# A kernel with a product-key expert layer: gates of all token groups made for all experts in one pass, their high and low parts laid out one behind the other

## The chip, the cores and the metric

The kernel runs on one core of a Trainium2 chip. The metric is the device time of one execution in microseconds. Of the kernel before there are three timed runs (1705.65, 1706.34 and 1710.72 us, median 1706.34) and one profiled execution of 1709.14 us, whose trace gives all rows below.

## The reference

One sequence of 256 tokens with 1024 features goes through a first block (a recurrent mixer, then an expert layer) and a second one (two layers of attention and a gated feed-forward). Only the expert layer matters here:

```
q     = t @ w_q                          # 256 tokens, 8 heads, 2 halves of 128
s, i  = top_k(q . sub_keys, 16)          # per half: 16 of 128 keys
idx   = i1 * 128 + i2  of the 16 best sums per head       # 128 experts per token, of 16384
g     = softmax(best)
out_p = sum over (h, k) of  g * gelu(u_tab[idx] . t_p) * v_tab[idx]
```

The kernel does not gather. It computes gelu(u . t) for all 16384 experts and all 256 tokens, multiplies by a gate that is zero where an expert was not chosen, and multiplies the result by all of v_tab. An expert is named by two numbers, i1 (0 to 127) and i2 (0 to 127): block i of the tables holds the 128 experts with i1 = i, and i2 is the partition.

## The kernel before, in words

**Weights.** All matrices come as 128x1024 fp32 tiles in one fixed list (`order`), 533 in all, each by one DMA on SP's queue (`w_dma`, L181). Each is split in two: ACT copies it to a high part (`whi`, L206), DVE subtracts to get the low part (`wlo`, L207). A product then has three matmuls: high by high, low by high, high by low (`mm3` L226, `add_part` L251). `weight(key)` (L218) hands out the next tile and splits those that follow, up to three tiles ahead while the u blocks run.

**The order of the work.** Python emits the instructions, and a planner that simulates the engines at build time places them in each engine's queue; every queue then runs in order on the chip. `tc.issue_after(x)` keeps an instruction behind x. `pump_behind(n)` (L808) takes n steps of a background generator and keeps what it emits behind the latest split of a weight.

**The u stage** (L959 to L967). For each of 128 blocks i, `u_block(i)` makes u tile i: 24 matmuls of 256 columns into one PSUM bank, gelu by ACT, and the result goes to row i of H (128 x 128 x 256 fp32, in three tiles: rows 0 to 31, 32 to 63, 64 to 127). In the first half of this stage the background is the choice of the experts (`topk`). When it ends, at about block 60, the background becomes `gates()`, in `pace` steps per block.

**Gates.** For a group of TB = 8 tokens: `one_hot` (L866) makes two 0/1 tables on DVE in fp16, with the 128 chosen experts of a token on the partitions: `eb` says which i2 each has, `ea` which i1. `with_gates` (L875) multiplies `ea` by the gate of each chosen expert, kept as a high and a low fp16 part, into `ahl`. On TensorE, `eb` of one token is the stationary operand and `ahl` of that token the moving one; the product is the gate of all (i2, i1) of the token. Tokens lie in pairs (TI = 2) as the innermost index of these tables.

Before the change the 32 groups are treated in two ways. In `gates()` groups 0 to 15 (tokens 0 to 127) are made for all 128 rows i1, and groups 16 to 31 for rows 0 to 63 only. `ahl` is laid out [group of pairs, row, high/low, token of the pair]: for one token and one part, the moving columns lie 4 fp16 elements, 8 bytes, apart. High and low are two matmuls that add up in PSUM (L886). `gate_apply` (L888) takes the gates from PSUM to H: rows whose u block is already there are multiplied by DVE (L893), the others are written by ACT (L896), and `u_block` multiplies them later by DVE (L954). A group is three background steps (four for groups 0 to 15); the steps are spread over the blocks up to 125:

```python
pace = (3 * T // TB + GM + 1) / (125 - i)      # L966: 113 steps, GM = 16
```

**The v stage** (L968 to L1003). H rows are split pairwise into a high and a low part (`ring`, L337 by ACT and L338 by DVE) and multiplied by the v tiles: 12 matmuls of 512 columns per row into four accumulating banks (L255). The ring lies where the u stage's input `xn2h`, `xn2l` was. The background of its first 64 rows is `gates_rest()` (L921): groups 16 to 31 for rows 64 to 127. It makes `eb` again, makes the other half of `ea` and of `ahl`, and here one matmul takes high and low together (L933): 64 rows x 2 parts = 128 moving columns, 2 elements, 4 bytes, apart, not added up in PSUM. ACT takes the low half out (L935), DVE adds the high half (L937) and multiplies H (L939).

Of the kernel before, what the change touches and what calls it, by code (L numbers as in the profile page):

```python
# [10 lines left out]
F32 = mybir.dt.float32  # L11
F32R = mybir.dt.float32r
F16 = mybir.dt.float16
# [3 lines left out]
AF = mybir.ActivationFunctionType  # L17
OP = mybir.AluOpType
# [3 lines left out]
T = 256  # L22
# [6 lines left out]
GS = 1024.0  # L29
TB = 8  # L30
TI = 2
NW = 3
HV = 36
PK = 1.35
GM = 16
LEAD = 4
VN = {"d": 1, "f": 0}
UL = (2, 7, 12, 17)
# [21 lines left out]
def kernel(  # L60
# [25 lines left out]
    pe, dve, act, pool = nc.tensor, nc.vector, nc.scalar, nc.gpsimd  # L86
# [22 lines left out]
    pacc = Four()  # L109
# [121 lines left out]
    def bank(shape, name, dt=F32):  # L231
        return pw.tile(shape, dt, tag="w", name=name)
# [92 lines left out]
    def background(gen):  # L325
        bgs["gen"], bgs["acc"] = gen, 0.0

    def pump(n):
        bgs["acc"] += n
        while bgs["acc"] >= 1.0:  # L330
            bgs["acc"] -= 1.0
            if bgs["gen"] is None or next(bgs["gen"], bgs) is bgs:
                bgs["gen"], bgs["acc"] = None, 0.0
                return
# [32 lines left out]
    IN_H0 = ("x", "yb", "lru", "sg")  # L367
    gp = pctx.enter_context(tc.tile_pool(name="gp", bufs=2))
    sks = []
    for tag, n, b in (("eb", 4, 2), ("ea", 4, 1), ("gs", 4, 1)):  # L370
        for j in range(b):
            t = gp.tile([128, n, 128], F32, tag=tag, name=f"sk{tag}{j}", bufs=b)
            sks += [(t, q, len(sks)) for q in range(n)]
    with tc.tile_pool(name="b1", bufs=1) as b1, tc.tile_pool(name="w1", bufs=1) as w1:
# [9 lines left out]
        x = full("x")  # L384
# [36 lines left out]
        r = raws.pop(0)  # L421
# [42 lines left out]
        for c in range(8):  # L464
            if c >= XG:
# [7 lines left out]
                                     op0=OP.mult, op1=OP.subtract)  # L473
# [7 lines left out]
        o = _OFF["norm2_g"]  # L481
# [79 lines left out]
        for c in range(8):  # L561
            if c % 4 == 0:
                Wg = weight(("ax", c // 4))
            o = (c % 4) * 256
# [93 lines left out]
        for c in range(8):  # L658
# [3 lines left out]
                                     op1=OP.subtract)  # L662
# [4 lines left out]
    with pctx:  # L667
        hp = pctx.enter_context(tc.tile_pool(name="hp", bufs=1))
        iE = gp.tile([128, 128, TI], F16, name="iE", bufs=1)
        i1T = gp.tile([128, T], F16, name="i1T", bufs=1)  # L670
        i2T = gp.tile([128, T], F16, name="i2T", bufs=1)

        gT = gp.tile([128, T // TI, 2, TI], F16, name="gT", bufs=1)
# [139 lines left out]
        for c in range(17):  # L813
# [10 lines left out]
            if c >= 2 and c % 2 == 0 and c <= 16:  # L824
                k = c // 2 - 1
                t = gp.tile([128, T], F32, tag="ut", name=f"x2t{k}")
# [11 lines left out]

        Hs = []
        HR = (0, 32, 64, 128)  # L840
        ub = {"u": 0, "groups": 0}

        def H_part(k):
            while len(Hs) <= k:
# [5 lines left out]
        def H_rows(a, b):  # L850

            for k in range(3):
                lo, hi = max(a, HR[k]), min(b, HR[k + 1])
                if lo < hi:
                    yield H_part(k)[:, (lo - HR[k]) * T:(hi - HR[k]) * T].rearrange("p (i t) -> p i t", t=T), lo, hi - lo

        def H_at(i, n=1):
            return next(H_rows(i, i + n))[0]

        TG = TB // TI  # L860

        def spread(row, t0, n):

            return row[:, t0:t0 + TB].rearrange("p (g j) -> p g j", j=TI).unsqueeze(2).to_broadcast([128, TG, n, TI])

        def one_hot(t0, a, n):  # L866
            eb = gp.tile([128, TG, 128, TI], F16, tag="eb", name=f"eb{a}_{t0}", bufs=2)
            dve.tensor_tensor(eb, spread(i2T, t0, 128), iE.unsqueeze(1).to_broadcast([128, TG, 128, TI]),
                              op=OP.is_equal)
            ea = gp.tile([128, TG, n, TI], F16, tag="ea", name=f"ea{a}_{t0}", bufs=1)  # L870
            dve.tensor_tensor(ea, spread(i1T, t0, n),
                              iE[:, a:a + n, :].unsqueeze(1).to_broadcast([128, TG, n, TI]), op=OP.is_equal)
            return eb, ea

        def with_gates(t0, a, n, ea):  # L875
            ahl = gp.tile([128, TG, n, 2, TI], F16, tag="ahl", name=f"ahl{a}_{t0}")
            dve.tensor_tensor(ahl, ea.unsqueeze(3).to_broadcast([128, TG, n, 2, TI]),
                              gT[:, t0 // TI:t0 // TI + TG].unsqueeze(2).to_broadcast([128, TG, n, 2, TI]),
                              op=OP.mult)
            return ahl  # L880

        def gate_sums(gps, eb, ahl):
            for t in range(TB):
                g, j = t // TI, t % TI
                for q in range(2):
                    pe.matmul(gps[:, t, :], eb[:, g, :, j], ahl[:, g, :, q, j], start=q == 0, stop=q == 1)  # L886

        def gate_apply(gps, t0, a, b):  # L888

            m = min(max(ub["u"], a), b)  # L890
            for hv, r, n in H_rows(a, m):
                hv = hv[:, :, t0:t0 + TB]
                dve.scalar_tensor_tensor(hv, gps[:, :, r - a:r - a + n].rearrange("p t i -> p i t"), 1.0 / GS, hv,  # L893
                                         op0=OP.mult, op1=OP.mult)
            for hv, r, n in H_rows(m, b):
                act.activation(hv[:, :, t0:t0 + TB], gps[:, :, r - a:r - a + n].rearrange("p t i -> p i t"), AF.Copy,  # L896
                               scale=1.0 / GS)

        def gates():

            pend = None
            for k in range(T // TB):
                t0, n = k * TB, 128 if k < GM else 64
                eb, ea = one_hot(t0, 0, n)
                yield
                ahl = with_gates(t0, 0, n, ea)
                yield
                if k < GM:
                    yield
                gps = pacc.tile([128, TB, n], F32, tag="g", name=f"g{t0}")  # L910
                gate_sums(gps, eb, ahl)
                if pend:
                    gate_apply(*pend)
                    ub["groups"] += 1
                pend = (gps, t0, 0, n)
                yield
            gate_apply(*pend)
            ub["groups"] += 1
            yield

        def gates_rest():  # L921
            for t0 in range(GM * TB, T, TB):
                eb, ea = one_hot(t0, 64, 64)
                yield
                ahl = with_gates(t0, 64, 64, ea)
                yield

                gs = gp.tile([128, 64, TB], F32, tag="gs", name=f"gs{t0}", bufs=1)
                for h in range(2):
                    gps = bank([128, 4, 64, 2], f"h{t0}{h}")  # L930
                    for t in range(4):
                        g, j = (4 * h + t) // TI, t % TI
                        pe.matmul(gps[:, t], eb[:, g, :, j], ahl[:, g, :, :, j], start=True, stop=True)  # L933
                    gv = gps.rearrange("p t i q -> p q i t")
                    act.activation(gs[:, :, 4 * h:4 * h + 4], gv[:, 1], AF.Copy)  # L935
                    yield
                    dve.tensor_tensor(gs[:, :, 4 * h:4 * h + 4], gv[:, 0], gs[:, :, 4 * h:4 * h + 4], op=OP.add)  # L937
                hv = H_at(64, 64)[:, :, t0:t0 + TB]
                dve.scalar_tensor_tensor(hv, gs, 1.0 / GS, hv, op0=OP.mult, op1=OP.mult)  # L939
                yield  # L940

        def u_block(i):
            W = weight(("u", i))
            ps = bank([128, T], f"u{i}")
            if i < 12:
                proj(ps, W, x2h, x2l)
            else:
                proj(ps, W, xn2h, xn2l)
            h = H_at(i)[:, 0, :]
            n = TB * (ub["groups"] if i < 64 else min(ub["groups"], GM))  # L950
            if n:
                t = gp.tile([128, T], F32, tag="ut", name=f"ut{i}")
                act.activation(t[:, 0:n], ps[:, 0:n], AF.Gelu_apprx_tanh)  # L953
                dve.tensor_tensor(h[:, 0:n], t[:, 0:n], h[:, 0:n], op=OP.mult)  # L954
            if n < T:
                act.activation(h[:, n:], ps[:, n:], AF.Gelu_apprx_tanh)  # L956
            ub["u"] = i + 1

        pace = PK  # L959
        for i in range(128):  # L960
            u_block(i)
            pump_behind(pace)
            if bgs["gen"] is None and pace == PK:
                pacc.hold(2)
                background(gates())
                pace = (3 * T // TB + GM + 1) / (125 - i)  # L966
        pump(1000)  # L967
        pacc.hold()  # L968
        background(gates_rest())
        acc = new_acc("pv")  # L970
        pairs = {}
        ring = [xp.tile([128, 4, 2, T], F32R, name=f"ring{x}", tag="x" + x) for x in "hl"]
# [23 lines left out]
        n_v = next(i for i, o in enumerate(order) if o[0] == ("v", 0))  # L996
        w_stage(n_v + HV, [in_h0(j) for j in range(4)])
        for i in range(125):
            if i == 64:
                pump(1000)  # L1000
            p = gated(i)
            W = weight(("v", i))
            add_k(acc, W, p, i == 0, False)  # L1003
            pump(5 * (T // TB - GM) / 56)
        Hr = hp.tile([128, 8192], F32, tag="H1", name="Hr")
        hk = Hr[:, 0:2048].rearrange("p (a b) -> p a b", a=2)
        nc.sync.dma_start(Hr[:, 0:2048], hdram)
# [28 lines left out]
    with ExitStack() as b2ctx:  # L1036
# [348 lines left out]
        h, xh, xl = layer_norm(acc, tail, h3, 0, 1, rows1, scales=r3a)  # L1385
# [199 lines left out]
```

## Time and profile before

| | |
|---|---|
| median of three runs | 1706.34 us |
| profiled execution, span in the trace | 1709.14 us, 1707.4 us |
| TensorE (PE), VectorE (DVE), ScalarE (ACT) busy | 1666.7, 1229.4, 902.1 us |
| u stage with gates | 441.3 to 676.7 us |
| v stage with the rest of the gates | 676.7 to 845.5 us |

Times in the rows count from the start of the span. PE is the matmul stream of TensorE, PEld its loading of stationary operands. [...] L12 is line 12 of the code.

### The profile page before, as it was taken

What the parts mean: (1) busy time and instruction counts of PE and PEld (TensorE: products, weight loads), DVE (VectorE), ACT (ScalarE), POOL (GpSimd) and SP (SyncE); (2) the same over time, 40 slices, a digit from 0 to 9 for tenths busy, and PEclk for the clock granted to TensorE, in tenths of its full rate; (3) what the DMA queues carried; (4) which work ended last, traced back from release to release, by engine and by line L of the source; (5) the groups of instructions that cost most, each with busy time, mean ns of one, the idle gap of its engine ahead of it and who ended that gap; (6) DMA issues with size and microseconds to landing.
All of it is one profiled execution on the core that took longest, in us unless ns stands there. A gap on an engine that the chain in (4) does not pass through costs nothing.

```text
span 1707.4 us, 29521 instructions
## 1 busy us (share of the span) xinstructions
PE 1666.7 (98%) x11533; PEld 1525.5 (89%) x11533; DVE 1229.4 (72%) x2220; ACT 902.1 (53%) x1556; POOL 121.6 (7%) x104
## 2 busy tenths in 40 slices
PE   8999999999999999999999999989999999999997
PEld 8998899999999999777788888877999889889997
DVE  7969689989777878778755546776766665567665
ACT  6786565454544444545544444765655456555552
POOL 2013010113000000000000001331000000000000
PEclk9999999999999999999999999999999999999999
DMA  7655646665544454556766655633765554346551
GB/s 245 199 161 163 208 147 222 187 186 180 167 146 140 149 154 145 189 180 204 240 193 190 194 188 198 194 105 106 228 188 186 170 174 137 111 143 217 183 185 50
DMA packets 90284, 296.61 MB, mean 174 GB/s; under 512 B 9168, under 2 KB 20000, under 8 KB 89376
## 3 DMA queue, kind: packets, MB, share of 16 engines
q1 hardware_dynamic: 88800, 293.66, 54.4%
q8 instruction: 91, 1.49, 0.4%
q10 hardware_dynamic: 1344, 1.05, 0.2%
q14 instruction: 49, 0.40, 0.1%
HBM read 289.39 MB, written 3.19 MB: 171 GB/s over the span
## 4 chain that ended last, share of the span: by engine, by line
PE 87%; DVE 5%; ACT 4%; DMA 2%; issue 2%; POOL 1%; POOLq 0%; SPq 0%; ACTq 0%; DVEq 0%
PE pv L255 21%; PE u L229 7%; PE u L227 7%; PE u L228 7%; PE ff L255 6%; PE g L886 3%; PE fg L229 2%; PE fg L227 2%; PE fg L228 2%; PE fu L227 2%; PE fu L229 2%; PE fu L228 2%; DVE wlo L207 1%; PE dpv L255 1%; PE ul L1132 1%
## 5 line engine op out<-in xcount | busy, mean ns | idle before, releaser
L207 DVE TENSOR_TENSOR wlo<-raw,whi 128x1024 fp32r<-128x1024 f32 x383 | 475.2, 1242 | 201.3 <-ACT whi L206 197.2
L206 ACT ACTIVATE whi<-raw 128x1024 fp32r<-128x1024 f32 x383 | 405.2, 1059 | 227.0 <-PE pv L255 87.3
L207 DVE TENSOR_TENSOR W<-raw,W 128x1024 fp32r<-128x1024 f32 x150 | 186.1, 1243 | 122.8 <-ACT W L206 122.5
L227 PE MATMUL u<-xn2h,whi 128*128 128x256 f32 x928 | 263.4, 284 | 0.0
L229 PE MATMUL u<-xn2l,whi 128*128 128x256 f32 x928 | 263.1, 284 | 0.0
L228 PE MATMUL u<-xn2h,wlo 128*128 128x256 f32 x928 | 262.7, 283 | 0.0
L206 ACT ACTIVATE W<-raw 128x1024 fp32r<-128x1024 f32 x150 | 158.7, 1061 | 155.5 <-PE pv L255 53.9
L228 PEld LDWEIGHTS u<-xn2h,wlo 128*128 128x128 f32 x928 | 175.5, 189 | 0.0
L227 PEld LDWEIGHTS u<-xn2h,whi 128*128 128x128 f32 x928 | 175.3, 189 | 0.0
L229 PEld LDWEIGHTS u<-xn2l,whi 128*128 128x128 f32 x928 | 175.1, 189 | 0.0
L255 PE MATMUL pv<-W,ringh 128*128 128x512 f32 x384 | 106.3, 391 | 0.0
L956 ACT ACTIVATE H<-u 128x256 f32<-128x256 f32 (+13 forms) x128 | 44.2, 345 | 92.6 <-PE u L229 92.5
L255 PE MATMUL pv<-whi,ringh 128*128 128x512 f32 x288 | 91.8, 399 | 0.1
L255 PE MATMUL pv<-whi,ringl 128*128 128x512 f32 x288 | 91.7, 395 | 0.0
L255 PE MATMUL pv<-wlo,ringh 128*128 128x512 f32 x288 | 89.8, 395 | 0.0
L255 PEld LDWEIGHTS pv<-W,ringh 128*128 128x128 f32 x384 | 71.6, 188 | 14.9
L953 ACT ACTIVATE ut<-u 128x128 f32<-128x128 f32 (+15 forms) x62 | 15.4, 248 | 123.9 <-PE u L229 123.9
L255 PEld LDWEIGHTS pv<-whi,ringl 128*128 128x128 f32 x288 | 54.1, 188 | 12.8
L255 PEld LDWEIGHTS pv<-wlo,ringh 128*128 128x128 f32 x288 | 53.9, 188 | 12.6
L255 PEld LDWEIGHTS pv<-whi,ringh 128*128 128x128 f32 x288 | 53.1, 188 | 11.8 <-ACT ringh L337 0.3
L255 PE MATMUL ff<-W,fph 128*128 128x512 f32 x192 | 59.3, 398 | 1.1 <-ACT fph L337 1.1
L255 PE MATMUL pv<-W,ringl 128*128 128x512 f32 x192 | 59.3, 390 | 0.0
(863 smaller groups left out, 4351.0 us busy)
## 6 DMA issues: line engine op xcount, KB each, us to landing
raw<-in_uT_dram SPq DMA_DIRECT2D x128, 512.0 KB, 3.6
raw<-in_v_dram SPq DMA_DIRECT2D x128, 512.0 KB, 3.6
raw<-in_ff_in_dram SPq DMA_DIRECT2D x80, 512.0 KB, 3.6
raw<-in_w_in_dram SPq DMA_DIRECT2D x56, 512.0 KB, 4.1
raw<-in_ff_out_dram SPq DMA_DIRECT2D x44, 512.0 KB, 4.1
raw<-in_w_q_dram SPq DMA_DIRECT2D x16, 512.0 KB, 3.6
raw<-in_qkw_dram SPq DMA_DIRECT2D x16, 512.0 KB, 4.1
raw<-in_f_qk_dram SPq DMA_DIRECT2D x16, 512.0 KB, 4.3
```

The source lines that it names most:

```text
L206: st["hi"] = act.activation(hi, r, AF.Copy).ins
L207: st["lo"] = dve.tensor_tensor(lo, r, hi.bitcast(F32), op=OP.subtract).ins
L227: pe.matmul(o, w[0], x[0], start=start, stop=False, skip_group_check=True)
L228: pe.matmul(o, w[1], x[0], start=False, stop=False, skip_group_check=True)
L229: pe.matmul(o, w[0], x[1], start=False, stop=stop, skip_group_check=True)
L255: i = pe.matmul(acc[2 * tt + nh], x_[:, ts], w_[:, nh * 512:nh * 512 + 512], start=f, stop=l, skip_group_check=True)
L886: pe.matmul(gps[:, t, :], eb[:, g, :, j], ahl[:, g, :, q, j], start=q == 0, stop=q == 1)
L953: act.activation(t[:, 0:n], ps[:, 0:n], AF.Gelu_apprx_tanh)
L956: act.activation(h[:, n:], ps[:, n:], AF.Gelu_apprx_tanh)
L1132: done = pe.matmul(u, x_[:, k, ts], w_[:, ns], start=f, stop=l, skip_group_check=True).ins
```

## The change

`gates_rest()` goes. `gates()` makes every group for all 128 rows beside the u blocks. `ahl` becomes [group of pairs, high/low, row, token of the pair], so that the columns of one part lie 2 elements, 4 bytes, apart; high and low stay two matmuls that add up in PSUM. Every group has three steps, 97 steps in all. `u_block` multiplies the gates of all tokens that are ready (`ub["gated"]`), in every row; before, at most 128 tokens in rows from 64 on. The 2 KB tile of `gates_rest` keeps its place in the pool under another name.

```diff
@@ -32,7 +32,6 @@
 NW = 3
 HV = 36
 PK = 1.35
-GM = 16
 LEAD = 4
 VN = {"d": 1, "f": 0}
 UL = (2, 7, 12, 17)
@@ -367,7 +366,7 @@
     IN_H0 = ("x", "yb", "lru", "sg")
     gp = pctx.enter_context(tc.tile_pool(name="gp", bufs=2))
     sks = []
-    for tag, n, b in (("eb", 4, 2), ("ea", 4, 1), ("gs", 4, 1)):
+    for tag, n, b in (("eb", 4, 2), ("ea", 4, 1), ("sk", 4, 1)):
         for j in range(b):
             t = gp.tile([128, n, 128], F32, tag=tag, name=f"sk{tag}{j}", bufs=b)
             sks += [(t, q, len(sks)) for q in range(n)]
@@ -838,7 +837,7 @@
 
         Hs = []
         HR = (0, 32, 64, 128)
-        ub = {"u": 0, "groups": 0}
+        ub = {"u": 0, "gated": 0}
 
         def H_part(k):
             while len(Hs) <= k:
@@ -863,81 +862,50 @@
 
             return row[:, t0:t0 + TB].rearrange("p (g j) -> p g j", j=TI).unsqueeze(2).to_broadcast([128, TG, n, TI])
 
-        def one_hot(t0, a, n):
-            eb = gp.tile([128, TG, 128, TI], F16, tag="eb", name=f"eb{a}_{t0}", bufs=2)
-            dve.tensor_tensor(eb, spread(i2T, t0, 128), iE.unsqueeze(1).to_broadcast([128, TG, 128, TI]),
-                              op=OP.is_equal)
-            ea = gp.tile([128, TG, n, TI], F16, tag="ea", name=f"ea{a}_{t0}", bufs=1)
-            dve.tensor_tensor(ea, spread(i1T, t0, n),
-                              iE[:, a:a + n, :].unsqueeze(1).to_broadcast([128, TG, n, TI]), op=OP.is_equal)
-            return eb, ea
-
-        def with_gates(t0, a, n, ea):
-            ahl = gp.tile([128, TG, n, 2, TI], F16, tag="ahl", name=f"ahl{a}_{t0}")
-            dve.tensor_tensor(ahl, ea.unsqueeze(3).to_broadcast([128, TG, n, 2, TI]),
-                              gT[:, t0 // TI:t0 // TI + TG].unsqueeze(2).to_broadcast([128, TG, n, 2, TI]),
+        def one_hot(t0):
+            e = [gp.tile([128, TG, 128, TI], F16, tag=f"e{x}", name=f"e{x}{t0}", bufs=n) for x, n in (("b", 2), ("a", 1))]
+            for o, row in zip(e, (i2T, i1T)):
+                dve.tensor_tensor(o, spread(row, t0, 128), iE.unsqueeze(1).to_broadcast([128, TG, 128, TI]),
+                                  op=OP.is_equal)
+            return e
+
+        def with_gates(t0, ea):
+            ahl = gp.tile([128, TG, 2, 128, TI], F16, tag="ahl", name=f"ahl{t0}")
+            dve.tensor_tensor(ahl, ea.unsqueeze(2).to_broadcast([128, TG, 2, 128, TI]),
+                              gT[:, t0 // TI:t0 // TI + TG].unsqueeze(3).to_broadcast([128, TG, 2, 128, TI]),
                               op=OP.mult)
             return ahl
 
-        def gate_sums(gps, eb, ahl):
-            for t in range(TB):
-                g, j = t // TI, t % TI
-                for q in range(2):
-                    pe.matmul(gps[:, t, :], eb[:, g, :, j], ahl[:, g, :, q, j], start=q == 0, stop=q == 1)
-
-        def gate_apply(gps, t0, a, b):
-
-            m = min(max(ub["u"], a), b)
-            for hv, r, n in H_rows(a, m):
-                hv = hv[:, :, t0:t0 + TB]
-                dve.scalar_tensor_tensor(hv, gps[:, :, r - a:r - a + n].rearrange("p t i -> p i t"), 1.0 / GS, hv,
-                                         op0=OP.mult, op1=OP.mult)
-            for hv, r, n in H_rows(m, b):
-                act.activation(hv[:, :, t0:t0 + TB], gps[:, :, r - a:r - a + n].rearrange("p t i -> p i t"), AF.Copy,
-                               scale=1.0 / GS)
+        def gate_apply(gps, t0):
+
+            for a, b in ((0, ub["u"]), (ub["u"], 128)):
+                for hv, r, n in H_rows(a, b):
+                    hv, gv = hv[:, :, t0:t0 + TB], gps[:, :, r:r + n].rearrange("p t i -> p i t")
+                    if a:
+                        act.activation(hv, gv, AF.Copy, scale=1.0 / GS)
+                    else:
+                        dve.scalar_tensor_tensor(hv, gv, 1.0 / GS, hv, op0=OP.mult, op1=OP.mult)
+            ub["gated"] = t0 + TB
 
         def gates():
 
             pend = None
-            for k in range(T // TB):
-                t0, n = k * TB, 128 if k < GM else 64
-                eb, ea = one_hot(t0, 0, n)
+            for t0 in range(0, T, TB):
+                eb, ea = one_hot(t0)
                 yield
-                ahl = with_gates(t0, 0, n, ea)
+                ahl = with_gates(t0, ea)
                 yield
-                if k < GM:
-                    yield
-                gps = pacc.tile([128, TB, n], F32, tag="g", name=f"g{t0}")
-                gate_sums(gps, eb, ahl)
+                gps = pacc.tile([128, TB, 128], F32, tag="g", name=f"g{t0}")
+                for t in range(TB):
+                    g, j = t // TI, t % TI
+                    for q in range(2):
+                        pe.matmul(gps[:, t, :], eb[:, g, :, j], ahl[:, g, q, :, j], start=q == 0, stop=q == 1)
                 if pend:
                     gate_apply(*pend)
-                    ub["groups"] += 1
-                pend = (gps, t0, 0, n)
+                pend = (gps, t0)
                 yield
             gate_apply(*pend)
-            ub["groups"] += 1
             yield
-
-        def gates_rest():
-            for t0 in range(GM * TB, T, TB):
-                eb, ea = one_hot(t0, 64, 64)
-                yield
-                ahl = with_gates(t0, 64, 64, ea)
-                yield
-
-                gs = gp.tile([128, 64, TB], F32, tag="gs", name=f"gs{t0}", bufs=1)
-                for h in range(2):
-                    gps = bank([128, 4, 64, 2], f"h{t0}{h}")
-                    for t in range(4):
-                        g, j = (4 * h + t) // TI, t % TI
-                        pe.matmul(gps[:, t], eb[:, g, :, j], ahl[:, g, :, :, j], start=True, stop=True)
-                    gv = gps.rearrange("p t i q -> p q i t")
-                    act.activation(gs[:, :, 4 * h:4 * h + 4], gv[:, 1], AF.Copy)
-                    yield
-                    dve.tensor_tensor(gs[:, :, 4 * h:4 * h + 4], gv[:, 0], gs[:, :, 4 * h:4 * h + 4], op=OP.add)
-                hv = H_at(64, 64)[:, :, t0:t0 + TB]
-                dve.scalar_tensor_tensor(hv, gs, 1.0 / GS, hv, op0=OP.mult, op1=OP.mult)
-                yield
 
         def u_block(i):
             W = weight(("u", i))
@@ -947,7 +915,7 @@
             else:
                 proj(ps, W, xn2h, xn2l)
             h = H_at(i)[:, 0, :]
-            n = TB * (ub["groups"] if i < 64 else min(ub["groups"], GM))
+            n = ub["gated"]
             if n:
                 t = gp.tile([128, T], F32, tag="ut", name=f"ut{i}")
                 act.activation(t[:, 0:n], ps[:, 0:n], AF.Gelu_apprx_tanh)
@@ -963,10 +931,9 @@
             if bgs["gen"] is None and pace == PK:
                 pacc.hold(2)
                 background(gates())
-                pace = (3 * T // TB + GM + 1) / (125 - i)
+                pace = (3 * T // TB + 1) / (125 - i)
         pump(1000)
         pacc.hold()
-        background(gates_rest())
         acc = new_acc("pv")
         pairs = {}
         ring = [xp.tile([128, 4, 2, T], F32R, name=f"ring{x}", tag="x" + x) for x in "hl"]
@@ -996,12 +963,9 @@
         n_v = next(i for i, o in enumerate(order) if o[0] == ("v", 0))
         w_stage(n_v + HV, [in_h0(j) for j in range(4)])
         for i in range(125):
-            if i == 64:
-                pump(1000)
             p = gated(i)
             W = weight(("v", i))
             add_k(acc, W, p, i == 0, False)
-            pump(5 * (T // TB - GM) / 56)
         Hr = hp.tile([128, 8192], F32, tag="H1", name="Hr")
         hk = Hr[:, 0:2048].rearrange("p (a b) -> p a b", a=2)
         nc.sync.dma_start(Hr[:, 0:2048], hdram)
```

## Rows read from the trace of the kernel before

**Rows 1.** The page: busy time, share of the span, instructions of each engine

```profile
PE 1666.7 (98%) x11533; PEld 1525.5 (89%) x11533; DVE 1229.4 (72%) x2220; ACT 902.1 (53%) x1556; POOL 121.6 (7%) x104
```

**Rows 2.** Stretches: start and end, busy time (instructions) by engine, granted clock, DMA

```profile
core 0: us, PE busy (x) PEld busy (x) DVE busy (x) ACT busy (x) POOL busy (x), PEclk, DMA share, GB/s
300.00:350.00 50.00, 50.00 (x424) 50.00 (x423) 46.90 (x130) 23.61 (x36) 10.18 (x6) 1.00 0.61 190
441.30:676.70 235.40, 235.40 (x2099) 233.80 (x2097) 181.85 (x309) 98.02 (x209) 0.00 (x0) 1.00 0.48 149
640.00:676.00 36.00, 36.00 (x350) 35.72 (x350) 29.28 (x54) 14.87 (x31) 0.00 (x0) 1.00 0.52 158
676.70:845.50 168.80, 168.69 (x818) 134.15 (x817) 134.81 (x186) 91.09 (x128) 0.00 (x0) 1.00 0.62 191
```

**Rows 3.** Chain of waits, 441.3 to 676.7: shares; pieces (start, us, what)

```profile
by line: PE u L229 26.9%; PE u L228 26.9%; PE u L227 26.9%; PE g L886 19.3%
...
448.14 1.87 PE g L886 x16
...
574.71 1.87 PE g L886 x16
581.37 0.96 PE g L886 x16
...
600.68 0.97 PE g L886 x16
601.65 0.17 PE u L227
...
671.78 0.96 PE g L886 x16
```

**Rows 4.** Chain of waits, 676 to 845.5: shares; pieces

```profile
by line: PE pv L255 94.8%; PE h L933 4.4%; ACT ringh L337 0.4%; PE u L228 0.2%; PE u L227 0.1%; PE u L229 0.1%; issue 0.0%
...
676.87 0.64 ACT ringh L337
...
678.75 0.49 PE h L933 x8
...
842.11 0.25 PE h L933 x4
```

**Rows 5.** Line 956, 255 to 441.3: count, min/median/max ns, first and last start

```profile
L956 ACT ACTIVATE H<-u x61: 384/386/388, 267.9 to 438.8; 128x256 f32<-128x256 f32 x61
```

**Rows 6.** Timeline: start us, us, engine, line, operation [idle before]

```profile
441.32 0.68 DVE L868 TENSOR_TENSOR eb<-i2T,iE 128x1024 f16<-128x1024 f16 x1
441.92 0.68 DVE L871 TENSOR_TENSOR ea<-i1T,iE 128x1024 f16<-128x1024 f16 x1
...
460.01 1.22 DVE L877 TENSOR_TENSOR ahl<-ea,gT 128x2048 f16<-128x2048 f16 x1
461.15 1.22 DVE L207 TENSOR_TENSOR wlo<-raw,whi 128x1024 fp32r<-128x1024 f32 x1
462.29 0.75 DVE L893 SCALAR_TENSOR_TENSOR H<-g,H 128x256 f32<-128x256 f32 x2
...
463.72 2.03 PE L886 MATMUL g<-ahl,eb 128*128 128x128 f16 x16
...
667.73 0.29 DVE L954 TENSOR_TENSOR H<-ut,H 128x128 f32<-128x128 f32 x1
667.94 0.68 DVE L877 TENSOR_TENSOR ahl<-ea,gT 128x1024 f16<-128x1024 f16 x1
```

**Rows 7.** Waits, 441 to 680: who waited for whom, us, times, longest

```profile
DVE wlo L207 <- ACT whi L206: 33.9, 49, 2.4
DVE H L954 <- ACT ut L953: 21.2, 30, 1.2
```

**Rows 8.** Waits, 300 to 350

```profile
DVE wlo L207 <- ACT whi L206: 2.5, 5, 0.9
```

## The prediction

> **What bounds the kernel now.** I read the page first: TensorE is busy 98% of the span, VectorE (DVE) 72%, ScalarE 53% [rows 1]. A share over the whole span says little, so the second look is the table of stretches around the gates. [...] So in both stages TensorE sets the time, and what counts is what the gates cost in its stream. That is read from the chain of waits, the third look: u matmuls and gate matmuls alone make up the first stage, with the gates at 19.3% [rows 3], and in the second the gate matmuls hold 4.4% [rows 4]. The fourth look is at what DVE waits for, because the change puts work on it: there are 33.9 us of waits for the high part of a weight and 21.2 us for a gelu [rows 7].
>
> **Gate matmuls in the u stage.** A group is 16 matmuls. With 128 columns 8 bytes apart it takes 1.87 us of the chain, and there are 16 of these; with 64 columns 8 bytes apart 0.96, also 16 [rows 3]. The v stage has the shape that the change makes everywhere: 128 columns 4 bytes apart, 8 matmuls in 0.49 us, so 16 in 0.98 [rows 4]. That gives 117, 60 and 61 ns for one matmul. After the change all 32 groups are of the third kind, with one difference: its pairs add up in PSUM. The u matmuls add up in one bank too and take 0.12 us for 256 columns (66 blocks in 235.40 us less the 45.4 us of gates are 190.0 us, 1584 matmuls), 0.47 ns a column, as the 61 ns for 128 do; so I charge nothing for adding up. The first 16 groups save 16 x (1.87 - 0.98) = 14.2 us, the others lose 16 x 0.02 = 0.3: **-13.9 us**. The bounds of a new group are 0.96 (as many loads of the stationary operand, half the columns) and 1.87 (the layout does nothing); I take 0.98, the row of the same width and step.
>
> [...]
>
> **Gate matmuls in the v stage.** They go, 23 runs in the chain from 678.75 to 842.11: 4.4% of 168.8 us is **-7.4 us**. One run of eight lies beside the wait for the first ring tile (ScalarE, 0.64 us, which starts when the last u matmul has read the tile that the ring overwrites), so that wait stays and the run returns nothing [rows 4]. Also gone there are 16 groups of DVE and ScalarE work (tables, products, sums). TensorE did not wait for them, so they return nothing more.
>
> **DVE in the u stage.** This is the bill. I take distances from start to start. `eb` and a full `ea` take 0.60 each; `ahl` with 2048 elements 1.14; a weight's low part (1024 fp32 elements) 1.14, 0.08 under its shown duration; two pieces of gates on 256 elements 0.75 - 0.08, so 0.33 each; the product H<-ut with 128 tokens 0.21 [rows 6]. From 0.21 at 128 and 1.14 at 1024 elements I estimate 0.08 + 0.00104 per fp32 element. One u block takes (438.8 - 267.9) / 60 = 2.85 us without gates [rows 5]. Of the 128 blocks 61 are done when the first table is made [rows 5, 6], so the new pace is 97 steps over some 65 blocks, 1.49 a block, so a group comes every 2.0 blocks: 2.0 x 2.85 + 0.98 + 0.05 (the first u matmul after a group takes 0.17 us of the chain, not 0.12 [rows 3]) = 6.75 us of TensorE.
>
> DVE's share of that, per group: tables and `ahl` 2.34; the gates of r finished rows 0.33 + 0.33 + 0.08 + 0.0083 (r - 64); two low parts 2.28; two H products of n tokens 2 x (0.08 + 0.00104 n). At the first group (r 62, n 0) that is 5.4 us, 81%; in the middle (r 95, n 128) 6.0, 90%; at the last (r 127, n 248) 6.6, **98%**. Over the stage it is 74.9 + 32.0 + 66 x 1.14 + 66 x 0.21 = 196 us of 221. TensorE was not held up where DVE was busy 46.90 of 50 us, in the choice of the experts [rows 2], and there DVE's waits had shrunk to 2.5 us in 50 [rows 8]: with a queue behind it, DVE does not wait for ScalarE. Up to 94% therefore has a row and costs nothing. Only the last eight or so groups are above it, by up to 4% of 6.75 us, together 1.3 us; low parts made up to three tiles ahead, and some 2.5 us between the end of an `ahl` (461.23) and its matmuls (463.72) [rows 6], cover that. I charge **+1 us**. If the cover is gone, u matmuls stand behind the gate matmuls that wait for `ahl`, and every microsecond that DVE is late is lost.
>
> The new `ahl` is not in the trace as an operation. Its elements and type are those of the 1.14 us row, and `eb` too is made of operands spread over rows in pairs; so I take 1.14. The upper bound is the rate of the fp32 low part, 2.28, which would add 36 us to DVE; lower than 1.14 nothing suggests.
>
> **What costs nothing, and why.** ScalarE now writes the not yet finished rows of 32 groups instead of 16; it has 98.02 us of work in 235.40 [rows 2], and if DVE were in its way the low parts would come later, which is rival 1. No DMA is issued by the moved steps, so SP's queue keeps its order. Before the first v block the last gates must be in H: the steps end at block 125, two blocks or 5.7 us early, and the ring waits for the last u matmul anyway; without that cover it would cost one group's products, 1.3 us.
>
> Sum: -13.9 - 7.4 + 1 = -20.3 us. The profiled execution took 1709.1, so it would take 1688.8. It lies 2.8 above the median of the runs; from the median I predict **1686 us** for the changed kernel, with 1682 to 1690 as this case's own range (up to 3 us more back from the restarts after the 23 runs, up to 5 us of DVE lag).
>
> **Rivals.**
> 1. DVE becomes the bound and keeps its waits. If the 55 us of waits [rows 7] stay beside 196 us of work, the u stage takes 251 instead of 221 us: -21.3 + 30 = +9, so **1715 us**, slower. It decides as soon as 21 us more than TensorE's 221 are needed, that is if 46 of the 55 us stay. For it speaks the 98% at the end, and that ScalarE, which makes the high parts, now also writes gates behind DVE's in the same tiles. Against it: the 50 us at 94% with only 2.5 us of waits. Chance 0.06; a new `ahl` at the slow rate is in it (231 us of work with few waits: +10, about 1696, and with half the waits slower).
> 2. The layout does nothing, and the pair that adds up in PSUM costs the 117 ns. Then 32 groups at 1.87: 16 x (1.87 - 0.96) = +14.6, -7.4, +1: **1714 us**. Against it: the 64-column pairs do as well per column, which fits both, but the u matmuls add up at full rate. Chance 0.04.
> 3. DVE's lag reaches TensorE in the last third, where it has 94 to 98%: a third of the 55 us of waits is 18, and if 5 to 15 of these stay and hold TensorE up, the time is **1691 to 1701 us**. For it: the planner's order is fixed at build time, and a DVE that runs late finds gate matmuls already placed ahead of u matmuls. Chance 0.11.
> 4. More than I count: the 23 runs that break the pv stream cost more than their own time, 0.2 us each with what stands around them instead of 0.05, and DVE's lag costs nothing: 4 to 6 us more, about **1681 us**. The rows show no sign of it. Chance 0.04.
>
> **Numbers.** The forecast has 0.75. The range holds it, rivals 3 and 4: 1680 to 1701, with about 0.1 outside above and little below. A measurement of this kernel can tell 0.3%, 5.1 us, from no change. Faster: forecast, 3 and 4, and a little of 1, 0.90, less 0.02 for a rival 3 worse than priced, 0.88. Slower: rivals 1 and 2, 0.09. Same: 0.03.
>
> **What would show it.** The chain of the changed kernel should show groups of 16 gate matmuls at 0.98 us all through, no gate matmul in the v stage, a u stage that ends near 662 and a v stage that starts with the ring wait. DVE should be busy about 200 of some 221 us, its waits well under 55. TensorE should wait under 2 us in the u stage. The prediction is wrong if the groups take 1.87 (rival 2), or if TensorE waits for `ahl`, gates or low parts by more than 5 us (rivals 1 and 3).

## The result, and the profile after

The changed kernel takes **1684.06 us** (median of four runs, 1683.75 to 1685.6) against 1707.72 for the kernel before beside it: a ratio of 0.9865, 95% interval 0.9854 to 0.9877. The prediction was 1686, range 1680 to 1701, faster with 0.88. The profiled execution took 1683.96 us, 25.2 less than that of before.

The page of the changed kernel, first row, answers to [rows 1]; the stretches, with the same columns as [rows 2], show the u stage and its last third:

```profile
PE 1643.0 (98%) x11405; PEld 1506.3 (90%) x11405; DVE 1202.5 (71%) x2140; ACT 898.9 (53%) x1538; POOL 121.7 (7%) x104
```

```profile
441.00:661.00 220.00, 220.00 (x2096) 218.39 (x2094) 196.96 (x319) 104.34 (x227) 0.00 (x0) 1.00 0.52 159
...
600.00:640.00 40.00, 40.00 (x385) 39.74 (x384) 38.24 (x61) 18.26 (x42) 0.00 (x0) 1.00 0.52 156
```

TensorE has 128 matmuls fewer, the ones that the v stage had. In the u stage it is still never idle, with DVE busy 96% of the last full 40 us. The chain of waits (start, us, what) counts a matmul from its start to the next start: a u matmul 0.12 us of it, where its record lasts 0.28, and the last group 0.94, where the timeline below shows 1.10. It answers to [rows 3] and has 32 equal groups, the first, two from the middle and the last:

```profile
447.41 0.97 PE g L902 x16
...
574.89 0.95 PE g L902 x16
581.59 0.95 PE g L902 x16
...
656.81 0.94 PE g L902 x16
```

The waits from 440 to 661, which answer to [rows 7]:

```profile
ACT ut L921 <- PE u L228: 85.5, 61, 2.4
DVE wlo L206 <- ACT whi L205: 24.0, 36, 1.8
ACT H L885 <- DVE H L887: 23.0, 29, 1.1
ACT H L924 <- PE u L228: 8.6, 5, 2.6
DVE H L887 <- PE g L902: 0.6, 1, 0.6
```

No wait of TensorE is among them. DVE's 55 us of waits have become 24.6, and the gelu wait is gone. Three DVE groups show the bill (count, busy us and mean ns), the new `ahl` at the length of the old one of equal size (1220 ns in [rows 6]):

```profile
L874 DVE TENSOR_TENSOR ahl<-ea,gT 128x2048 f16<-128x2048 f16 x32 | 39.0, 1218 | 0.0
L868 DVE TENSOR_TENSOR ea<-i1T,iE 128x1024 f16<-128x1024 f16 x32 | 21.9, 684 | 0.0
L868 DVE TENSOR_TENSOR eb<-i2T,iE 128x1024 f16<-128x1024 f16 x32 | 21.8, 682 | 0.0
```

And the end of the u stage in the timeline (in brackets the idle time before, and what ended it):

```profile
656.65 1.10 PE L902 MATMUL g<-ahl,eb 128*128 128x128 f16 x16
...
657.79 1.34 DVE L887 SCALAR_TENSOR_TENSOR H<-g,H 128x256 f32<-128x256 f32 x3 [0.61 <-PE g L902]
...
659.61 0.17 ACT L885 ACTIVATE H<-g 128x16 f32<-128x16 f32 x1
...
660.93 1.15 ACT L336 ACTIVATE ringh<-H 128x512 fp32r<-128x512 f32 x2
...
661.62 1.19 PE L254 MATMUL pv<-whi,ringh 128*128 128x512 f32 x4 [0.60 <-ACT ringh L336]
...
663.17 0.73 PE L254 MATMUL pv<-whi,ringl 128*128 128x512 f32 x2 [0.36 <-DVE ringl L337]
```

The last gates are in H at 659.8, only some 1.2 us before the ring could start anyway.

Where the time went, profile against profile: the gelu of the last plain u block starts 0.7 us earlier (438.8 to 438.1); from there to the first ring tile 238.1 us became 222.8, 15.2 less; from there to the first transpose behind the v stage 363.8 became 355.7, 8.1 less; the other 1.3 us of the span's 25.3 lie behind it, where nothing was changed. The u stage ends at 660.9; the prediction said near 662.

### The profile page after: what moved, and what is told of

It is laid out like the page before. It is cut to its first block, busy times and chain, and to the rows that moved or that the text cites. A ratio compares the mean times of both kernels' runs of the same rounds, so it can differ in the third digit from the quotient of the medians.

```text
span 1682.1 us, 29153 instructions
## 1 busy us (share of the span) xinstructions
PE 1643.0 (98%) x11405; PEld 1506.3 (90%) x11405; DVE 1202.5 (71%) x2140; ACT 898.9 (53%) x1538; POOL 121.7 (7%) x104
## 4 chain that ended last, share of the span: by engine, by line
PE 87%; DVE 5%; ACT 4%; DMA 2%; issue 2%; POOL 1%; POOLq 0%; ACTq 0%; SPq 0%; DVEq 0%
PE pv L254 21%; PE u L226 7%; PE u L228 7%; PE u L227 7%; PE ff L254 7%; PE fg L226 2%; PE fg L227 2%; PE fg L228 2%; PE fu L226 2%; PE fu L228 2%; PE fu L227 2%; PE g L902 2%; DVE wlo L206 1%; PE ul L1096 1%; PE wo L254 1%
## 5 line engine op out<-in xcount | busy, mean ns | idle before, releaser
L924 ACT ACTIVATE H<-u 128x256 f32<-128x256 f32 (+30 forms) x126 | 41.9, 332 | 93.7 <-PE u L228 93.6
L254 PEld LDWEIGHTS pv<-W,ringh 128*128 128x128 f32 x384 | 72.1, 188 | 15.2
L921 ACT ACTIVATE ut<-u 128x8 f32<-128x8 f32 (+30 forms) x62 | 17.2, 277 | 85.5 <-PE u L228 85.5
```

Of the source, the lines that this page charges most:

```text
L254: i = pe.matmul(acc[2 * tt + nh], x_[:, ts], w_[:, nh * 512:nh * 512 + 512], start=f, stop=l, skip_group_check=True)
```

## The experiments

Each ratio is to the kernel before, timed beside it. The changed kernel, timed again (`after_again`), gave 1682.79.

| kernel | us | ratio, 95% interval |
|---|---|---|
| layout_only | 1685.08 | 0.9868 (0.9852 to 0.9885) |
| one_pass_only | 1713.22 | 1.0034 (1.0022 to 1.0045) |
| ahl_twice | 1713.41 | 1.0036 (1.0021 to 1.0050) |
| eb_twice | 1698.00 | 0.9942 (0.9925 to 0.9958) |
| ea_once | 1683.10 | 0.9850 (0.9833 to 0.9866) |
| no_low | 1678.99 | 0.9836 (0.9820 to 0.9853) |
| high_only | 1670.17 | 0.9776 (0.9760 to 0.9792) |
| after_again | 1682.79 | 0.9855 (0.9839 to 0.9872) |
| first_rows_apart | 1682.53 | 0.9854 (0.9837 to 0.9870) |
| old_layout_no_add, fours_8_bytes, fours_16_bytes | 1714.08, 1711.46, 1792.52 | one run each |

**The two halves of the change, each alone.** `layout_only` is the kernel before with this in `gates()`:

```diff
-  ahl = gp.tile([128, TG, n, 2, TI], ...)      # in gates() only; gates_rest() as it was
+  ahl = gp.tile([128, TG, 2, n, TI], ...)
-  pe.matmul(gps[:, t, :], eb[:, g, :, j], ahl[:, g, :, q, j], ...)
+  pe.matmul(gps[:, t, :], eb[:, g, :, j], ahl[:, g, q, :, j], ...)
```

> The kernel before with the new layout of ahl in the u stage alone (both the groups of 128 rows and those of 64); the rest of the gates stays in the v stage with its old layout. Theory (the step between moving columns sets a gate matmul's time): the 16 groups of 128 rows fall from 1.87 to about 0.96 us, 14.6 us less, about 1693 us where the kernel before takes 1707.7. The 16 groups of 64 rows tell what is under the columns: still about 0.96 if the load of the stationary operand holds 60 ns, about 0.5 (7 us more, 1686) if columns alone count. Rival (the pair that adds up in PSUM costs the time, not the layout): groups stay at 1.87, no change, 1708.

Measured: 1685.08 us, the whole gain. Its chain of waits has the 128-row groups first, then the 64-row groups, then the rest in the v stage:

```profile
446.71 0.97 PE g L886 x16
...
559.17 0.95 PE g L886 x16
564.91 0.50 PE g L886 x16
...
649.05 0.51 PE g L886 x16
...
655.58 0.49 PE h L940 x8
```

The 64-row groups fell from 0.96 to 0.50. So a matmul of 64 columns took 31 ns with its load of the stationary operand (0.50 us / 16), and the 0.96 of [rows 3] was the old step as well. `one_pass_only` is the changed kernel with `ahl` back in [.., row, high/low, token]:

> The changed kernel with ahl in the old layout, 8 bytes between moving columns: all 32 groups for all rows in the u stage. Theory: each group takes 1.87 instead of 0.96 us, 32 x 0.91 = 29 us more than the changed kernel, about 1713 us, which is 5 us slower than the kernel before; DVE then has more room (about 197 us of work in 250). Rival (the layout does nothing, the gain comes from one pass): as the changed kernel, about 1684.

Measured: 1713.22, as the theory has it, slower than the kernel before. All complete groups in its chain are like these:

```profile
454.66 1.87 PE g L902 x16
...
678.23 1.87 PE g L902 x16
```

**Step or adding up?** Three kernels, one run each. `old_layout_no_add` is `one_pass_only` with `start=True, stop=True` in both matmuls, so that the high part of the gates is left out; `fours_8_bytes` is the changed kernel, and `fours_16_bytes` is `one_pass_only`, with `TI = 4` (tokens in fours, which also puts the stationary columns 8 bytes apart instead of 4).

> The changed kernel with the old layout, and with both matmuls of a pair starting anew in PSUM, so that the low part alone is left and the high part of the gates is left out. Theory (the step of the moving columns): groups of 1.87 us as in the kernel before, about 1713 us. Rival (adding up in PSUM costs the time): groups of about 0.96 us, about 1684 us.

> The changed kernel with tokens in fours instead of pairs as the innermost index (TI = 4): the layout stays high behind low, but the columns of one token lie 8 bytes apart in both operands. Theory (8 bytes between columns are read at half the rate): groups of about 1.87 us, about 1713 us. Rival (the order of high and low matters, not the step): 0.96 us, 1684.

> Tokens in fours and the old layout (row, high/low, token): moving columns 16 bytes apart, stationary ones 8. Theory A (the rate falls with the step, 4 bytes a column being free): 3.6 us a group, 85 us more than the changed kernel, about 1769 us. Theory B (anything beyond 4 bytes costs a factor of two once): 1.87 us, about 1713 us.

Measured: 1714.08, 1711.46 and 1792.52. A group in the chain of each, in this order:

```profile
454.89 1.87 PE g L902 x16
```

```profile
453.56 1.90 PE g L902 x16
```

```profile
454.98 3.70 PE g L902 x16
```

Without adding up the old layout still takes 1.87, and the new order of high and low with 8 bytes between columns takes 1.90: it is the step. It is that of the moving operand: with the stationary columns at 4 bytes (`old_layout_no_add`) and at 8 (`fours_8_bytes`) a group takes nearly the same. At 16 bytes it doubles again, so theory A held. The 87 us of the gate matmuls (32 x (3.69 - 0.96)) would have given 1771; the run took 21 us more, and in its u stage the granted clock is 0.89 to 0.92, although TensorE is never idle there. Behind many groups it is 0.50, and the u matmuls take 0.21 us each instead of 0.12:

```profile
560.00:620.00 60.00, 60.00 (x381) 50.52 (x380) 35.63 (x60) 18.84 (x42) 0.00 (x0) 0.89 0.34 104
...
479.20:481.00 1.80, 1.80 (x10) 1.80 (x10) 0.00 (x1) 0.00 (x0) 0.00 (x0) 0.50 0.72 257
```

```profile
475.00 0.12 PE u L226
...
475.48 3.69 PE g L902 x16
479.17 0.21 PE u L227
479.38 0.22 PE u L228
```

That is where the 21 us lie: in the chain from 441 to 770 the 1574 u matmuls take 211 us, and at the changed kernel's 0.121 us each they would take 190.

**How hidden is DVE?** Two kernels add DVE work to the changed kernel (a second, equal `dve.tensor_tensor` behind the one of `eb`, or of `ahl`), one takes work away (`ea` of the first group serves all).

> The changed kernel with each eb written twice: 0.60 us of DVE work more per group, 19 us in the stage. Theory: DVE's 197 us become 216 in a stage of 221; the first half of the groups still has room, the second half is over by up to 0.45 us a group, 4 us in all, of which the lead of the splits hides 2 to 3: 1684 to 1688 us. Rival (DVE's waits for ScalarE and the fixed order make its last 10% unusable): TensorE loses 8 us or more, above 1692.

> The changed kernel with each ahl written twice by the same product: 1.14 us of DVE work more per group, 36.5 us in the stage, nothing else. Theory (DVE is hidden only up to its own limit, and the changed kernel has some 24 us of room left in the u stage): DVE's 197 us become 233 in a stage of 221, so TensorE must wait 12 to 18 us, about 1697 to 1702 us. Rival A (DVE has no part in the time at all, the planner moves its work away): 1684. Rival B (DVE keeps its waits for ScalarE): 24 to 30 us, 1708 to 1714.

> The changed kernel with ea made for the first group alone and used by all others (the other 31 tables of i1 are left out, so the gates land in wrong rows): 0.60 us of DVE work less per group, 19 us in the stage, nothing else. Theory (the changed kernel is still set by TensorE, DVE hidden with about 5 us to spare): no gain, 1683 to 1685 us, with more of DVE's time in waits. Rival (DVE is what sets the changed kernel's u stage): it gains 5 us or more, under 1679.

Measured: 1698.00, 1713.41, 1683.10. Taking 19 us of DVE work away gains nothing, so DVE does not set the changed kernel. But of the 19 us that `eb_twice` adds, 14 arrive in the time, and of the 36.5 of `ahl_twice` 29: by the time the room is 5 to 7 us and not the 24 that DVE's idle time suggested. Both expectations were too low; for both kernels the figure of the rival that lets DVE keep its waits fits. The timeline of `eb_twice` (as above) shows where most of it is collected, and its waits up to 661 what DVE kept:

```profile
664.84 1.51 PE L905 MATMUL g<-ahl,eb 128*128 128x128 f16 x16 [1.92 <-DVE ahl L877]
670.20 1.89 PE L905 MATMUL g<-ahl,eb 128*128 128x128 f16 x16 [3.85 <-DVE ahl L877]
674.89 1.22 PE L254 MATMUL pv<-whi,ringh 128*128 128x512 f32 x2 [2.81 <-ACT H L888]
```

```profile
DVE wlo L206 <- ACT whi L205: 10.8, 19, 1.8
```

The gates slide back behind the u blocks, which costs little until these end: up to 661 TensorE is busy 216.94 of 220.00 us. But row 0 of H is whole only when the last group is in, so the first v block cannot start, and TensorE stands still for the last two `ahl` and for the last gates. DVE's waits for the high part of a weight are still 10.8 us, of 24.0 in the changed kernel.

Before the end TensorE is held up through ScalarE: a u matmul waits until the gelu of an earlier block has emptied a PSUM bank, and that gelu stands in ScalarE's queue behind other work. The first rows are these waits in `eb_twice` and in `ahl_twice` (whose profiled run lies 5 us above its median); the timeline shows one of the latter, behind a gate write for which ScalarE waited on DVE:

```profile
PE u L226 <- ACT H L927: 3.1, 2, 1.5
...
PE u L226 <- ACT H L927: 12.7, 6, 4.9
```

```profile
594.36 0.34 ACT L888 ACTIVATE H<-g 128x208 f32<-128x208 f32 x1 [2.94 <-DVE H L890]
...
595.62 0.58 PE L226 MATMUL u<-xn2h,whi 128*128 128x256 f32 x1 [4.59 <-ACT H L927]
```

The stretches of `eb_twice` show TensorE untouched, then held up, and the granted clock falling at the end:

```profile
560.00:600.00 40.00, 40.00 (x384) 39.78 (x382) 37.66 (x61) 17.65 (x39) 0.00 (x0) 1.00 0.54 169
600.00:640.00 40.00, 38.47 (x362) 38.03 (x361) 37.33 (x58) 17.54 (x41) 0.00 (x0) 1.00 0.51 158
...
661.00:675.00 14.00, 5.43 (x50) 4.70 (x48) 12.02 (x21) 4.51 (x11) 0.00 (x0) 0.66 0.29 94
```

And the stage up to the first v matmul, in the changed kernel, `eb_twice`, `ahl_twice` and `no_low` (below):

```profile
441.00:661.60 220.60, 220.01 (x2096) 218.39 (x2094) 197.56 (x320) 104.94 (x228) 0.00 (x0) 1.00 0.51 159
...
441.00:674.90 233.90, 222.27 (x2100) 219.80 (x2098) 218.57 (x355) 105.37 (x231) 0.00 (x0) 0.98 0.50 154
...
441.00:693.90 252.90, 230.11 (x2116) 226.97 (x2114) 237.78 (x355) 107.77 (x232) 0.00 (x0) 0.95 0.47 145
...
441.00:654.60 213.60, 205.04 (x1835) 203.13 (x1834) 198.74 (x321) 105.14 (x230) 0.00 (x0) 0.99 0.58 168
```

DVE is idle for 23 us of the stage in the changed kernel, and for 15 us in each of the three where it holds TensorE up. So 15 us could not be used, and the room is some 8 us of DVE work. The time shows less room: in `eb_twice` TensorE's waits grow by 10.7 us (11.7 against 1.0), and the other 3 of the 14 us I estimate from the timeline around the stretch with a mean granted clock of 0.66: the last group loses 0.8 us (1.89 against 1.10), and the first v matmuls, 0.43 us apart until 678.5 instead of 0.23, lose 2.

**Less on TensorE.** `no_low` has `for q in range(1)` in the matmuls; `high_only` also makes `ahl` of the high part alone, [group of pairs, row, token], 1024 elements.

> The changed kernel without the low part's matmul (the product of the low part of the gates is left out); DVE still makes both parts. Theory (TensorE sets the time, and a gate matmul costs 60 ns on it): 256 matmuls less, 15.3 us; DVE's 197 us then stand against 205, with the last third of the groups above 100%, which gives back 1 to 4 us: 1669 to 1673 us. Rival (DVE is already the hidden bound of the changed kernel): less than 5 us gained, above 1679.

> The changed kernel with gates as one fp16 number: the low part of the gates is left out on TensorE and in DVE's product, which has 1024 elements instead of 2048. TensorE has 15.3 us less, DVE 0.54 us a group or 17 us less. Theory (leaving out the low matmul alone gained 5 of its 15 us because DVE, with only some 5 us to spare, then set the end of the stage): with DVE relieved too the whole 15.3 us come, 1668 to 1670 us. Rival (the other 10 us were lost to something else, as the start of the v stage): it stays at 1675 or above.

Measured: 1678.99 and 1670.17. In `no_low` 15.3 us leave TensorE and 5 come out, less than expected; its u stage ends as that of `eb_twice` does, with the same 15 us of idle DVE time, and the room read from its time is again 5 us:

```profile
646.03 0.64 PE L902 MATMUL g<-ahl,eb 128*128 128x128 f16 x8 [1.64 <-DVE ahl L874]
650.79 1.01 PE L902 MATMUL g<-ahl,eb 128*128 128x128 f16 x8 [4.12 <-DVE ahl L874]
654.61 1.22 PE L254 MATMUL pv<-whi,ringh 128*128 128x512 f32 x2 [2.80 <-ACT H L885]
```

In `high_only`, where DVE is relieved by 17 us too, nearly all comes: 1684 - 1670 is 14 of 15.3. It beats both kernels, for the price of gates kept as one fp16 number.

**The start of the v stage.** `first_rows_apart` splits rows 0 and 1 into tiles of the gates' pool (`if 0 < i < 120` in `gated`), so that they need not wait for the last u matmul.

> The changed kernel once more, beside the next one on the same chip: 1684 us, 23 to 24 us under the kernel before.

> The changed kernel, with the high and low parts of H rows 0 and 1 in tiles of the gates' pool (as rows 120 to 127 have them) instead of in the ring, which lies on the input of the u blocks. In the changed kernel TensorE stands still 0.60 us for the first ring tile and 0.36 us for its low part. Theory (the wait comes from the place that the ring shares): both go, 0.9 us less, about 1683 us, hardly to be told from the changed kernel by its time but by those two waits. Rival (the splits are late for another cause, the gates or the queue of DVE): the waits stay, no change.

Measured: 1682.79 and 1682.53. The two waits are gone, and the v matmuls follow the last u matmul at once:

```profile
661.29 0.28 PE L228 MATMUL u<-xn2l,whi 128*128 128x256 f32 x1
661.41 1.09 PE L254 MATMUL pv<-whi,ph 128*128 128x512 f32 x4
...
662.33 0.62 PE L254 MATMUL pv<-whi,pl 128*128 128x512 f32 x2
```

The time cannot tell 0.9 us.

## Why the prediction was right, point by point

- **TensorE sets both stages.** Before the change it was busy 235.40 of 235.40 us in the u stage and 168.69 of 168.80 in the v stage, at a granted clock of 1.00 [rows 2]. Shown for the u stage: `ea_once` takes DVE work away without gain (1683.10 us), `high_only` takes TensorE work away and gains it (14 of 15.3 us). In the v stage the gain of 8.1 us where gate matmuls of 7.4 us went agrees.
- **Gate matmuls of the u stage, -13.9 us.** Right. The 32 groups sum to 30.7 us in the chain against 45.4 before, -14.7. A new group takes 0.94 to 0.97 us, not 0.98. That adding up in PSUM cost nothing is shown by `old_layout_no_add`, with 1.87 us a group as in `one_pass_only`. Rival 2 fell: a group takes 0.96 us at 4 bytes, 1.87 to 1.90 at 8, 3.7 at 16.
- **What lies under the columns.** Wrong in a detail that the sum hid. I read the 0.96 of the 64-row groups as what the loads of stationary operands leave, a lower bound of a new group; `layout_only` shows 0.50. So it was not two savings of 14 and 7 us, one by the layout and one by the single pass. The layout alone brings 22 us, the single pass alone costs 6, and on top of the layout it brings 1 to 2, which the runs cannot tell from nothing: a full group at 0.96 costs TensorE what two halves at 0.50 and 0.98 / 2 cost.
- **Gate matmuls of the v stage, -7.4 us.** 8.1 measured between the points given above; rival 4 wanted some 3.5 us more here. The ring wait stayed, 0.60 + 0.36 us, as the step said, and `first_rows_apart` shows that it hangs on the shared place and can be had.
- **DVE in the u stage, +1 us.** The work was sized rightly, 196 us against 196.96 busy, and so was the new `ahl` (1218 ns). The cost was 0 to 1 us: TensorE waits for DVE nowhere in the stage. But the cover was not the one I named. I trusted the lead of the splits and two blocks of time at the end; the trace has the last gates in H 1.2 us before the ring, and three experiments give 5 to 7 us of room by the time, some 8 us of DVE work. That the term came out near nothing was a closer thing than the sum shows. Beyond that edge rivals 1 and 3 have the mechanism in part: DVE does not keep all its waits, but 15 of its 23 idle us stay idle, its lag reaches TensorE through ScalarE's gelus, and the rest of the bill falls due at the end of the stage, where H must be whole. How much of those 15 us the fixed order makes and how much ScalarE's own queue was not separated.
- **Sum.** -20.3 predicted, -23.7 between medians. Of the 3.4 us, 0.8 are the groups, 0.7 the v stage and 1 DVE; about 1 is left, less than the 2.0 by which the two profiles differ in stretches where nothing was changed. That 1686 came within 2 us of 1684.06 is partly luck: the sum was taken from a median of 1706.34, and the kernel before took 1707.72 beside the changed one.

## What to carry to other kernels

Look at the step between the columns of a moving operand before counting matmuls: here 128 fp16 columns took 60, 117 and 231 ns at 4, 8 and 16 bytes, and swapping two axes of a table brought what the whole change brought. A term that a layout and a restructuring share should be tried one by one, because the cost of the old structure may itself be the layout's. And the idle time of a hidden engine is no measure of its room: here 15 of 23 us could not be used. Work that must be complete at a stage's end has only the time that its last piece is early, here 1.2 us, and before that its lag can travel through the queue of a third engine, here ScalarE's, for which TensorE waited 3.1 us in `eb_twice` and 12.7 in `ahl_twice`.

## What the runs showed of the hardware that was not expected

- The cost of a moving column went with its step over the whole range tried: 0.47 ns at 4 bytes (0.96 us / 16 / 128), 0.91 at 8, 1.81 at 16, each about 0.11 to 0.12 ns a byte. A step of 2 bytes was not tried. The loads of stationary operands, one for each matmul, hid under it down to 64 columns at 4 bytes, 31 ns a matmul and 0.49 ns a column in `layout_only`.
- Where TensorE stood still at the stage's end, its granted clock was lower too: a mean of 0.66 over 661 to 675 in `eb_twice`, busy 5.43 of 14.00 us, against 1.00 in the changed kernel, busy 13.04 there. The group at 670.20 takes 1.89 us in the timeline where the last one of the changed kernel takes 1.10. So the stop cost more than its own length. With a step of 16 bytes the granted clock fell to a mean of 0.89 with TensorE shown busy all the time, and what paid were the u matmuls behind the slow groups, 0.21 us each at 0.50 against 0.12 at 1.00.
